# A seventeenth block pair: half of q's projection moved from plain matmuls to seven block products

## The chip, the cores and the metric

The kernel runs on one core of one Trainium2 chip. The metric is the device time of one execution in microseconds (us), as the median of several runs. The profile comes from one further execution, recorded by the hardware profiler.

## What is computed

One layer of a hybrid encoder on 1024 positions of width 1024, in float32. Cut to what matters here:

```python
h = layer_norm(x, emb_ln_g, emb_ln_b)
proj = h @ w_in                       # 1024 x 5120
q, k, v, z_a, u, z_b, g_a, g_b = split(proj)   # q, k, v, z_a, u, z_b: 512 columns each, g_a, g_b: 1024
attn = neighbourhood_attention(q * HEAD_DIM ** -0.5, k, v, rpb)
y_a = attn * silu(z_a)
hh = rg_lru(conv(u), forward) + rg_lru(conv(u), backward)
y_b = hh * silu(z_b)
m = sigmoid(g_a + b_a) * (y_a @ w_ba) + sigmoid(g_b + b_b) * (y_b @ w_bb)
out = layer_norm(ALPHA * h + m @ w_out)
```

The change concerns the projection `h @ w_in`, and of it the 512 columns of q: four column tiles of 128, numbered 0 to 3. The factor 0.125 (HEAD_DIM ** -0.5) is applied when q leaves PSUM.

## The kernel before, in words

**Exact products from two halves.** TensorE works on float32 operands that are rounded to its float32r form. So each operand is split into a high part (a rounding cast) and a low part (the operand less its high part), and a product is the sum of three matmuls: high by high, low by high, high by low (`mm3`, L134). The cast is usually ScalarE's, the subtraction (`lo_of`, L128) VectorE's or GpSimd's.

**Stages.** (1) Eight position tiles of 128 are loaded, normalized, transposed on TensorE and split into the four blocks B11, B12, B21, B22 of the transposed input (the first index is the half of the 1024 input features, the second the half of the 1024 positions). Their block sums T1 to T4 are built from the second half's tiles 4 to 7: `t_full` and `t_last` make them on VectorE (L302 to L310), `t_hi` casts them on ScalarE (L314), `t_lo` makes the low halves on GpSimd (`ht_l<-t,ht_h` in the profile). The block sums lie in a ring of five places of 4 KB per partition (tag `x`) that the loaded tiles used before. (2) In between, V is computed (`v_part`, L328: 24 matmuls for a position tile), stored by `v_hi`, `v_lo`, `v_store`, and q by `q_part(m, n)`: column tile m, position half n, 24 matmuls of 512 columns. `qk_load`, `qk_prep` (`qk_hi` on ScalarE, `qk_lo` on GpSimd) bring the weights of a column tile of q; `q_hi` (ScalarE), `q_lo` (VectorE, L360) and `q_store` bring a finished part away. (3) All other column tiles but V's go through 16 pairs. A pair is two column tiles that are computed together by a Strassen-like scheme: seven block products (`OPS`) of 4 x 3 = 12 matmuls in place of eight. A pair p needs four weight blocks a11, a21, a12, a22 (`s_load`), four sums of them s1 to s4 (`s_sum`, on VectorE, both inputs in SBUF), and high and low parts of seven operands (`s_hi`, `s_lo`). (4) Convolution and gates of the recurrent branch run between the products of the pairs; (5) attention, the two branch products, the output product and the last normalization follow.

**What sets the order.** TensorE, VectorE, ScalarE, GpSimd and SyncE (which issues the DMAs) each execute in the order in which the program issues. In the stage of pairs the order is a table: slot `7 * p + k` holds product k of pair p, with the evacuation of the product before it, the preparation of the next pair and what `todo` holds for that slot (`CONV_AT`, `GATE_AT`, `LATE_AT`, `HEAD_AT` are slot numbers). `evacuate` copies PSUM results to SBUF (u1, u2, u3, on ScalarE) and adds others to them (VectorE); a `take` function per pair says where the four results go: `take_u` for u, `take_zg` for gates, `take_k` for k. A product that accumulates into a PSUM bank waits until the results in it have been read. `U_PAIRS` are the pairs whose last sum goes straight into an SBUF tile, so that they need no fourth bank.

**The boundary.** After V's last part the kernel before computes q(0,1), q(1,1), q(2,0), q(2,1), q(3,0), q(3,1), in this order. Pair 0's loads, sums and splits stand among these six. Then the pools of the first stages are released, VectorE computes a small chain of 128 x 8 operations (a softplus of the recurrence's parameter, L626 to L642, with one ScalarE activation, L629, for which a table is loaded), and pair 0's first product begins. Tile 7's `t_hi` and `t_lo` stand behind q(0,1) and the preparation of q's column tile 2. V's weights lie in the places of the pairs' split operands, so pair 0's high and low parts can't be written before V's last part.

Of the kernel before, what the change touches and what calls it, by code (L numbers as in the profile page):

```python
# [10 lines left out]
F32 = mybir.dt.float32  # L11
F32R = mybir.dt.float32r
AF = mybir.ActivationFunctionType
ALU = mybir.AluOpType

P = 128
# [7 lines left out]
HALF = 512  # L24
# [1 line left out]
EPS = 1e-5  # L26
TWICE = 4.0
C_LRU = 8.0
N_PAIR = 16


WARM = 18, 4, 6
CONV_AT = (7, 24, 45, 66)
GATE_AT = (14, 24, 35, 45, 56, 66, 77, 87)
LATE_AT = (102, 102, 103, 104, 105)
HEAD_AT = 109
LO_POOL = ("a11", "a22")
HI_POOL = ("a12", "s2", "s1", "s3", "s4")
U_PAIRS = (0, 5)
BLOCKS = (1, 0, 6, 2, 3, 4, 5, 7)  # L40
SCORES = (0, 1, 2, 5, 6, 7, 3, 4)
PV_LAG = 3
# [25 lines left out]
def encoder_kernel(ctx, tc, x, gb1, gb, w_qk, w_v, w_s, w_ba, w_bb, w_gate, smalls, bias, w_out, out):  # L68
    nc = tc.nc
    V, A, G, PE, SP = nc.vector, nc.scalar, nc.gpsimd, nc.tensor, nc.sync  # L70
# [10 lines left out]
    wsp = pool("wsp")  # L81
# [15 lines left out]
    q_d = dram.tile([H // 2, P, 2, S], F32, name="q_d")  # L97
    k_d = dram.tile([H // 2, P, 2, S], F32, name="k_d")
    rs_d = dram.tile([H, NT, P], F32, name="rs_d")
    za_d = dram.tile([4, P, S], F32, name="za_d")  # L100
    zb_d = dram.tile([4, P, S], F32, name="zb_d")
# [25 lines left out]
    def lo_of(eng, lo, full, hi):  # L127
        eng.tensor_tensor(lo, full, hi.bitcast(F32), ALU.subtract)  # L128
# [16 lines left out]
    OPS = ("a11", "a12", "s2", "s1", "s3", "s4", "a22")  # L145
    INTO = dict(s2="a11", s3="a11", a22="a11", s4="s1")
    wpl = pool("wpl", "right")
    ln = pool("ln", "right")
# [16 lines left out]
    def qk_load(m):  # L165
        qk_s[m] = wpl.tile([P, NK, P], F32, tag="ws", bufs=1, name=f"wqk{m}_s")
        SP.dma_start(qk_s[m][:], w_qk[m])
# [9 lines left out]
    def qk_prep(m):  # L177
        qk_hi(m)
        qk_lo(m)
# [25 lines left out]
    halves = [slice(c * HALF, (c + 1) * HALF) for c in range(2)]  # L205
# [86 lines left out]
    def t_full(i):  # L292

        tt[i, 3] = wsp.tile([P, 4, P], F32, tag="a22", bufs=2, name=f"t3_{i}")[:]
        t12 = ln.tile([P, 2, 4, P], F32, tag="x", bufs=5, name=f"t12_{i}")
        tt[i, 1], tt[i, 2] = t12[:, 0], t12[:, 1]
        if i in (4, 6):
            tt["last"] = ln.tile([P, 2, 4, P], F32, tag="x", bufs=5, name=f"t4_{i}")
        tt[i, 4] = tt["last"][:, i % 2]
        t1, t2, t3 = (tt[i, c] for c in (1, 2, 3))  # L300
        A.copy(t3, tp4(i, 0))
        V.tensor_tensor(t1, tp4(i, 0), f(B11[0], i), ALU.subtract)  # L302
        V.tensor_tensor(t1, t1, f(B11[1], i), ALU.subtract)
        V.tensor_tensor(t2, tp4(i, 1), t1, ALU.subtract)
        V.tensor_tensor(t3, tp4(i, 1), t3, ALU.subtract)
# [6 lines left out]
    def t_hi(i, *cs):  # L312
        for c in cs:
            A.copy(Ts[c][0][:, :, ti(i)], tt[i, c])  # L314

    def t_lo(i, *cs):
        for c in cs:
            lo_of(G, Ts[c][1][:, :, ti(i)], tt[i, c], Ts[c][0][:, :, ti(i)])
# [3 lines left out]
    def v_part(i, kind, ks):  # L322

        if i not in vos:
            vos[i], vn[i] = bank(f"v{i}"), 0
        for k in ks:
            a = blocks[k // 4][i // 4][kind == "a"][:, k % 4, ti(i)]
            PE.matmul(vos[i][:], a, wv[kind == "w"][k][:], start=vn[i] == 0, stop=vn[i] == 23)  # L328
            vn[i] += 1
# [3 lines left out]
    def v_hi(i):  # L333
        vs = outs["v", i] = ln.tile([P, H, 2, DH], F32R, tag="vs", bufs=2, name=f"vs{i}")
        A.copy(vs[:, :, 0, :], vos[i][:].rearrange("p (h d) -> p h d", d=DH))
# [11 lines left out]
    def q_part(m, n, cols=slice(0, HALF)):  # L347
        if (m, n) not in qos:
            qos[m, n] = bank(f"q{m}_{n}")
        run(mm3(qos[m, n][:, cols], [([t[:, 4 * kk + k, :] for t in qk_w[m]], [t[:, k, cols] for t in blocks[kk][n]])  # L350
                                     for kk in range(2) for k in range(4)]))

    def q_hi(m, n):
        qs = outs["q", m, n] = ln.tile([P, 2, HALF], F32R, tag="vs", bufs=2, name=f"q{m}{n}")
        A.activation(qs[:, 0, :], qos[m, n][:], AF.Copy, scale=0.125)

    def q_lo(m, n):

        qs = outs["q", m, n]
        V.scalar_tensor_tensor(qs[:, 1, :], qos.pop((m, n))[:], 0.125, qs[:, 0, :].bitcast(F32), ALU.mult, ALU.subtract)  # L360

    def q_store(m, n):
        qs = outs.pop(("q", m, n))
        SP.dma_start(q_d[m][:, :, halves[n]], qs[:].bitcast(F32))


    s_a, s_w = {}, {}

    def s_load(p, *names):
        for o in names if p < N_PAIR else ():  # L370
            t = wsp.tile([P, 4, P], F32, tag=o, bufs=2 if o == "a22" else 1, name=f"{o}_{p}f")
            SP.dma_start(t[:], w_s[p, ("a11", "a21", "a12", "a22").index(o)])
            s_a[p, o] = t

    def s_sum(p, *names):
        for o in names if p < N_PAIR else ():
            a, b, op = dict(s1=("a21", "a22", ALU.add), s2=("s1", "a11", ALU.subtract),
                            s3=("a11", "a21", ALU.subtract), s4=("a12", "s2", ALU.subtract))[o]
            t = s_a[p, o] = wsp.tile([P, 4, P], F32, tag=o, name=f"{o}_{p}f")
            V.tensor_tensor(t[:], s_a[p, a][:], s_a[p, b][:], op)  # L380

    def s_hi(p, o):
        if p < N_PAIR:
            s_w[p, o] = pair(wsp, [P, 4, P], f"w{o}_{p}", tag="w" + o)
            (G.tensor_copy if p and o in HI_POOL else A.copy)(s_w[p, o][0][:], s_a[p, o][:])

    def s_lo(p, o):
        if p < N_PAIR:
            hi, lo = s_w[p, o]
            lo_of(G if o in LO_POOL else V, lo[:], s_a[p, o][:], hi[:])  # L390


    K0, K1, KS, BOTH = range(4), range(4, 8), range(8), range(2)
# [136 lines left out]
    v_lo(2)  # L530
    v_store(2)
    keep(5)
    qk_load(2)
    tile_in(4)
    tile_lo(4)
    ln_next(7)
# [41 lines left out]
    t_last(6)  # L578
    t_hi(6, 4)
    t_lo(6, 4)  # L580
    t_full(7)
    for kind in "hwa":
        v_part(6, kind, KS)
# [3 lines left out]
    v_store(6)  # L587
    for kind in "hwa":
        v_part(7, kind, KS)
    v_hi(7)  # L590
    v_lo(7)
    v_store(7)
    s_load(0, "a11")
    for m in range(4):
        for n in BOTH if m > 1 else (1,):
            q_part(m, n)
            if m < 2:
                qk_prep(m + 2)
                if m == 0:
                    qk_load(3)  # L600
                    t_hi(7, 2, 1, 3, 4)
                    t_lo(7, 2, 1, 3, 4)
                    s_load(0, "a21", "a22", "a12")
                else:
                    s_sum(0, "s1", "s2", "s3", "s4")
            q_hi(m, n)
            q_lo(m, n)
            q_store(m, n)
            if m > 1:
                for w in (OPS[:2], OPS[2:4], OPS[4:6], OPS[6:])[2 * (m - 2) + n]:  # L610
                    s_hi(0, w)
                    s_lo(0, w)
    s_load(1, "a11", "a21", "a12", "a22")
    for pl in (ln, wpl, hb12, pst, ps0):
        pl.release()
    psd = tc.alloc_tile_pool(name="psd", bufs=1, space=bass.MemoryType.PSUM, reuse_waits="tile")
# [29 lines left out]
    def take_u(m0):  # L646
        for m in (m0, m0 + 1):
            up = lru.tile([P, S + 3], F32, tag="up", bufs=2, name=f"up{m}")
            V.memset(up[:, 0:2], 0.0)
            V.memset(up[:, S + 2:S + 3], 0.0)  # L650
            ups[m] = up

        def consume(mi, n, add, o):
            dst = gridded(ups[m0 + mi][:, 2:2 + S], n)
            if add is None:
                A.copy(dst, tiled(o[:], 0))
            else:
                V.tensor_tensor(dst, tiled(add[:], 0), tiled(o[:], 0), ALU.add)
            return []
        return consume  # L660

    def take_zg(dst, m0, name, col=None):

        def consume(mi, n, add, o, c=None):
            c = o if c is None else c
            if add is not None:
                V.tensor_tensor(c[:], add[:], o[:], ALU.add)
            z = ev.tile([P, HALF], F32, tag="z", bufs=5, name=f"{name}{m0}{mi}{n}")

            def squash():  # L670
                bias = {} if col is None else dict(bias=smh[:, col + m0 + mi:col + m0 + mi + 1])
                A.activation(z[:], c[:], AF.Tanh, scale=0.5, **bias)

            def store():
                if col is None:
                    V.scalar_tensor_tensor(z[:], z[:], 1.0, c[:], ALU.add, ALU.mult)
                SP.dma_start(dst[m0 + mi][:, n * HALF:(n + 1) * HALF], z[:])
            return [squash, store]
        return consume

    def take_k(m0):
# [216 lines left out]
    def gates_a(j):  # L898
        return lambda: take_zg(ga_d, 2 * j, "ga", SM_BM)

    def gates_b(j):
        return lambda: take_zg(gb_d, 2 * j, "gb", SM_BM + 8)

    takes = [lambda: take_u(0), lambda: take_zg(zb_d, 0, "zb"), lambda: take_zg(za_d, 0, "za"), gates_a(0), gates_a(1),
             lambda: take_u(2), gates_b(0), lambda: take_zg(zb_d, 2, "zb"), gates_a(2), gates_b(1),
             lambda: take_k(0), gates_a(3), lambda: take_k(2), lambda: take_zg(za_d, 2, "za"), gates_b(2), gates_b(3)]
    for t, slot in enumerate(CONV_AT):
# [444 lines left out]
    for i in range(NT):  # L1352
        last = i == NT - 1
        load_z(i + 3)
        z = zs.pop(i)
# [115 lines left out]
```

## Time and profile before

| | us |
|---|---|
| median of 3 runs | 678.17 (678.04 to 678.44) |
| the profiled execution's own time | 678.46 |
| its span, first to last instruction | 676.7 |
| mean granted TensorE clock | 0.997 |

In the profile, PE is TensorE, DVE VectorE, ACT ScalarE, POOL GpSimd, and SPq the queue of SyncE. A row of the timeline has the start in us from the span's beginning, the length in us, engine, line, operation, `out<-in` by the program's names without their numbers, the form, a count, and in brackets the engine's idle time before it with what ended it. Rows of one form that follow each other are merged (x4). A row of waits has the engine and the line that waited, whom it waited for, the total in us, the count and the longest. The chain in order of time lists the work that set the end, piece by piece. A row of the windows has, for a stretch, the busy time of TensorE, its weight loads, VectorE, ScalarE and GpSimd, then the granted clock, the DMA share and GB/s.

### The profile page before, as it was taken

How to read it: one execution, taken by the hardware profiler on the slowest of the kernel's cores; microseconds unless marked ns; L12 is line 12 of the kernel's file. 1: busy time of each engine (PE TensorE's matmuls, PEld its weight loads, DVE VectorE, ACT ScalarE, POOL GpSimd, SP SyncE). 2: the span in 40 equal slices, each digit the busy share in tenths (PEclk: the TensorE clock that was granted, in tenths of full speed). 3: DMA queues.
4: the chain of work that ended last, by engine and by line, in shares of the span. 5: the costliest groups of instructions: out<-in, count | busy, mean ns of one | idle time of the engine just before them, and what ended most of it. 6: DMA issues, size and time to landing. Idle time of an engine off the chain costs nothing.

```text
span 676.7 us, 9344 instructions
## 1 busy us (share of the span) xinstructions
PE 665.2 (98%) x3201; PEld 555.7 (82%) x3201; DVE 492.7 (73%) x821; ACT 364.5 (54%) x612; POOL 355.8 (53%) x258
## 2 busy tenths in 40 slices
PE   8999999999999999999999999999999999999995
PEld 6888888888888887888788888888888878888884
DVE  6978747886998699879967785477787787443434
ACT  6554433256786676669576634477777554210110
POOL 6798632434677576567647444116155456334442
PEclk9999999999999999999999999999999999999998
DMA  8654353233434133431553456998793467412211
GB/s 326 244 179 170 122 206 126 77 110 123 125 128 144 40 103 115 170 126 48 195 178 122 173 191 254 316 366 296 255 323 132 162 220 281 178 62 94 93 63 62
DMA packets 48702, 113.39 MB, mean 168 GB/s; under 512 B 5056, under 2 KB 9744, under 8 KB 47120
## 3 DMA queue, kind: packets, MB, share of 16 engines
q1 hardware_dynamic: 48624, 112.81, 47.2%
q8 instruction: 25, 0.41, 0.3%
q14 instruction: 21, 0.17, 0.1%
q10 hardware_dynamic: 32, 0.01, 0.0%
HBM read 77.11 MB, written 35.68 MB: 167 GB/s over the span
## 4 chain that ended last, share of the span: by engine, by line
PE 89%; DVE 6%; DMA 2%; issue 1%; SPq 1%; ACT 0%; POOL 0%; DVEq 0%; POOLq 0%
PE a L134 30%; PE o L134 13%; PE mb L134 12%; PE s L134 11%; PE q L134 6%; PE v L328 6%; PE acc L1107 3%; PE s L1061 3%; PE pt L1083 3%; PE g L759 2%; DMA wqk_s<-in_w_qk_dram 2%; DVE ws_l L128 1%; PE tp L270 1%; DMA rsb<-rs_d 1%; DVE uc L717 1%
## 5 line engine op out<-in xcount | busy, mean ns | idle before, releaser
L134 PE MATMUL o<-wo_h,ml 128*128 128x512 f32 (+1 forms) x136 | 51.2, 377 | 0.0
L134 PE MATMUL o<-wo_l,mh 128*128 128x512 f32 (+1 forms) x136 | 51.2, 376 | 0.0
L134 PE MATMUL o<-wo_h,mh 128*128 128x512 f32 (+1 forms) x136 | 51.2, 376 | 0.0
L134 PE MATMUL a<-ht_h,ws_h 128*128 128x512 f32 x128 | 50.0, 390 | 0.0
L134 PE MATMUL a<-ht_l,ws_h 128*128 128x512 f32 x128 | 49.8, 389 | 0.0
L134 PE MATMUL a<-ht_h,ws_l 128*128 128x512 f32 x128 | 49.8, 389 | 0.0
L134 PE MATMUL a<-b_h,wa_h 128*128 128x512 f32 x128 | 49.8, 389 | 0.0
L134 PE MATMUL a<-b_h,wa_l 128*128 128x512 f32 x128 | 49.8, 389 | 0.0
L134 PE MATMUL a<-b_l,wa_h 128*128 128x512 f32 x128 | 49.8, 389 | 0.0
L1071 DVE CUSTOM_DVE_ANT_0 sc<-s,bias 128x384 f32<-128x384 f32 (+1 forms) x64 | 33.4, 522 | 21.6 <-PE s L1061 14.2
L1361 DVE SCALAR_TENSOR_TENSOR z<-z,o 128x512 f32<-128x512 f32 (+1 forms) x17 | 11.2, 656 | 51.0 <-PE o L134 51.0
L1091 ACT CAST pt_h<-pt 128x384 fp32r<-128x384 f32 x64 | 29.0, 453 | 25.3 <-PE pt L1083 17.3
L1371 POOL TENSOR_TENSOR z<-z,gb 128x1024 f32<-128x1024 f32 x7 | 16.8, 2400 | 48.5 <-ACT z L1370 48.5
L1076 ACT ACTIVATE p<-sc,summ 128x384 f32<-128x384 f32 (+1 forms) x64 | 37.8, 591 | 5.5 <-DVE summ L1071 5.3
L1340 ACT ACTIVATE sd<-mv,eps_z 128x1 f32<-128x1 f32 x8 | 2.4, 294 | 67.1 <-DVE mv L1366 67.1
L128 DVE TENSOR_TENSOR pt_l<-pt,pt_h 128x384 fp32r<-128x384 f32 x64 | 33.2, 519 | 2.1 <-ACT pt_h L1091 1.6
L328 PE MATMUL v<-wv,b_h 128*128 128x512 f32 x128 | 32.9, 398 | 0.6 <-ACT b_h L279 0.5
L867 POOL CAST wb_h<-wb 128x512 fp32r<-128x512 f32 x9 | 7.0, 779 | 47.4 <-DMA wb<-in_w_bb_dram 47.4
L1061 PE MATMUL s<-ks,qs 128*128 128x384 f32 (+1 forms) x128 | 31.4, 327 | 0.0
L1083 PEld LDWEIGHTS pt<-ident,p 128*128 128x128 f32 x176 | 23.1, 140 | 8.5
L1083 PE MATMUL pt<-ident,p 128*128 128x128 f32 x176 | 29.6, 272 | 0.0
L128 POOL TENSOR_TENSOR wb_l<-wb,wb_h 128x512 fp32r<-128x512 f32 x16 | 22.0, 1375 | 14.3 <-ACT wb_h L865 13.6
(438 smaller groups left out, 2204.2 us busy)
## 6 DMA issues: line engine op xcount, KB each, us to landing
ks<-k_d SPq DMA_DIRECT2D x8, 1024.0 KB, 7.5
h_d<-x SPq DMA_DIRECT2D x8, 512.0 KB, 5.0
v_d<-vs SPq DMA_DIRECT2D x8, 512.0 KB, 3.7
q_d<-q SPq DMA_DIRECT2D x8, 512.0 KB, 3.1
ga_d<-ga SPq DMA_DIRECT2D x16, 256.0 KB, 2.2
gb_d<-gb SPq DMA_DIRECT2D x16, 256.0 KB, 2.6
k_d<-k SPq DMA_DIRECT2D x8, 512.0 KB, 3.4
qs<-q_d SPq DMA_DIRECT2D x8, 512.0 KB, 5.5
```

The source lines that it names most:

```text
L128: eng.tensor_tensor(lo, full, hi.bitcast(F32), ALU.subtract)
L134: PE.matmul(o, a, b, start=first and i == 0, stop=last and i == len(prods) - 1, skip_group_check=not (first and last))
L328: PE.matmul(vos[i][:], a, wv[kind == "w"][k][:], start=vn[i] == 0, stop=vn[i] == 23)
L759: PE.matmul(o[:, n, :], w[:, 2 * d + b, :], us[b][:, n * HALF:(n + 1) * HALF], start=z == 0, stop=z == 1)
L1061: PE.matmul(o[:, :P * len(near(t))], q[:, t * P:(t + 1) * P], k[:, z, keys], start=z == 0, stop=z == 1)
L1071: V.tensor_tensor_reduce(s[:, :w], o[:, :w], heads[h][2][:, b0:b0 + w], -1.0, 3.0e38, ALU.add, ALU.min, accum_out=sums[h][0][:, t:t + 1])
L1076: A.activation(probs[h % 2][t][:], scs.pop((h, t))[:, :w], AF.Exp, bias=sums[h][0][:, t:t + 1], scale=-1.0, accum_out=sums[h][1][:, t:t + 1])
L1083: PE.transpose(tp[:, n * P:(n + 1) * P], probs[h % 2][t][:, z * P:(z + 1) * P], ident[:])
L1091: A.copy(pt[0][:, span(b)], tps[h, b][:, :P * len(near(b))])
L1107: PE.matmul(acc[g][:, d:d + w], vvs[h // 2][:, b, h % 2, :], pt[:, a:a + w], start=b in (1, 6) and z == 0, stop=z == 1 and b == (4, 7)[g])
L1361: V.scalar_tensor_tensor(z[:, cols], z[:, cols], ALPHA * TWICE, o, ALU.mult, ALU.add)
L1371: G.tensor_tensor(z[:], z[:], gb2[:, 0, :], ALU.mult)
```

## The change

q's column tiles 2 and 3 are no longer computed by four `q_part`s of 24 matmuls. They become a pair of their own, with seven products of 12 matmuls, ahead of the sixteen. All slot numbers of the table grow by 7, the pairs' numbers by 1. The new pair 0's weight blocks are loaded earlier, two at a time, into places of the ring `x` (places of dead block sums); the loads of the old pair 0, now pair 1, move up as well. All of the new pair 0's sums, casts and low halves stand within q(0,1) and q(1,1); casts are ScalarE's and low halves VectorE's for this pair. Tile 7's `t_hi` and `t_lo` now stand ahead of `v_hi(7)`. A new `take_q` scales the four results and stores them as `q_store` did.

```diff
-N_PAIR = 16
+N_PAIR = 17
-CONV_AT = (7, 24, 45, 66)
+CONV_AT = (14, 31, 52, 73)
...
-U_PAIRS = (0, 5)
+U_PAIRS = (1, 6)
...
     def s_load(p, *names):
-        for o in names if p < N_PAIR else ():
-            t = wsp.tile([P, 4, P], F32, tag=o, bufs=2 if o == "a22" else 1, name=f"{o}_{p}f")
-            SP.dma_start(t[:], w_s[p, ("a11", "a21", "a12", "a22").index(o)])
+        for z, o in enumerate(names if p < N_PAIR else ()):
+            if p:
+                t = wsp.tile([P, 4, P], F32, tag=o, bufs=2 if o == "a22" else 1, name=f"{o}_{p}f")[:]
+            else:
+                if z == 0:
+                    both = ln.tile([P, 2, 4, P], F32, tag="x", bufs=5, name=f"{o}_{p}f")
+                t = both[:, z]
+            SP.dma_start(t, w_s[p, ("a11", "a21", "a12", "a22").index(o)])
...
-            lo_of(G if o in LO_POOL else V, lo[:], s_a[p, o][:], hi[:])
+            lo_of(G if p and o in LO_POOL else V, lo[:], s_a[p, o], hi[:])
...
     keep(5)
-    qk_load(2)
     tile_in(4)
...
     t_hi(6, 4)
     t_lo(6, 4)
+    s_load(0, "a21", "a22")
+    s_load(0, "a11", "a12")
+    s_load(1, "a21", "a12")
     t_full(7)
...
     for kind in "hwa":
         v_part(7, kind, KS)
+    t_hi(7, 2, 1, 3, 4)
+    t_lo(7, 2, 1, 3, 4)
     v_hi(7)
     v_lo(7)
     v_store(7)
-    s_load(0, "a11")
-    for m in range(4):
-        for n in BOTH if m > 1 else (1,):
-            q_part(m, n)
-            if m < 2:
-                qk_prep(m + 2)
-                if m == 0:
-                    qk_load(3)
-                    t_hi(7, 2, 1, 3, 4)
-                    t_lo(7, 2, 1, 3, 4)
-                    s_load(0, "a21", "a22", "a12")
-                else:
-                    s_sum(0, "s1", "s2", "s3", "s4")
-            q_hi(m, n)
-            q_lo(m, n)
-            q_store(m, n)
-            if m > 1:
-                for w in (OPS[:2], OPS[2:4], OPS[4:6], OPS[6:])[2 * (m - 2) + n]:
-                    s_hi(0, w)
-                    s_lo(0, w)
-    s_load(1, "a11", "a21", "a12", "a22")
+    s_load(1, "a11")
+    s_load(1, "a22")
+    q_part(0, 1)
+    s_sum(0, "s1", "s2", "s3", "s4")
+    for o in OPS[:3]:
+        s_hi(0, o)
+        s_lo(0, o)
+    q_hi(0, 1)
+    q_lo(0, 1)
+    q_store(0, 1)
+    q_part(1, 1)
+    for o in OPS[3:]:
+        s_hi(0, o)
+        s_lo(0, o)
+    q_hi(1, 1)
+    q_lo(1, 1)
+    q_store(1, 1)
...
+    def take_q():
+
+        def consume(mi, n, add, o, c=None):
+            c = o if c is None else c
+            if add is not None:
+                V.tensor_tensor(c[:], add[:], o[:], ALU.add)
+            t = lru.tile([P, 2, HALF], F32R, tag=("us0", "r", "i", "us1")[2 * mi + n], name=f"q2{mi}{n}")
+
+            def high():
+                A.activation(t[:, 0, :], c[:], AF.Copy, scale=0.125)
+
+            def store():
+                V.scalar_tensor_tensor(t[:, 1, :], c[:], 0.125, t[:, 0, :].bitcast(F32), ALU.mult, ALU.subtract)
+                SP.dma_start(q_d[2 + mi][:, :, halves[n]], t[:].bitcast(F32))
+            return [high, store]
+        return consume
...
-    takes = [lambda: take_u(0), lambda: take_zg(zb_d, 0, "zb"), lambda: take_zg(za_d, 0, "za"), gates_a(0), gates_a(1),
+    takes = [take_q, lambda: take_u(0), lambda: take_zg(zb_d, 0, "zb"), lambda: take_zg(za_d, 0, "za"), gates_a(0), gates_a(1),
...
-    heads = [16, 20, 12, 24, 26, 18, 32, 22, 28, 34, 4, 30, 6, 14, 36, 38]
+    heads = [2, 16, 20, 12, 24, 26, 18, 32, 22, 28, 34, 4, 30, 6, 14, 36, 38]
```

More of the change, by code (lines that the diff above doesn't have):

```diff
@@ L28 @@
 C_LRU = 8.0
-N_PAIR = 16
+N_PAIR = 17
 WARM = 18, 4, 6
-CONV_AT = (7, 24, 45, 66)
-GATE_AT = (14, 24, 35, 45, 56, 66, 77, 87)
-LATE_AT = (102, 102, 103, 104, 105)
-HEAD_AT = 109
+CONV_AT = (14, 31, 52, 73)
+GATE_AT = (21, 31, 42, 52, 63, 73, 84, 94)
+LATE_AT = (109, 109, 110, 111, 112)
+HEAD_AT = 116
 LO_POOL = ("a11", "a22")
 HI_POOL = ("a12", "s2", "s1", "s3", "s4")
-U_PAIRS = (0, 5)
+U_PAIRS = (1, 6)
 BLOCKS = (1, 0, 6, 2, 3, 4, 5, 7)
@@ L378, in s_sum @@
                             s3=("a11", "a21", ALU.subtract), s4=("a12", "s2", ALU.subtract))[o]
-            t = s_a[p, o] = wsp.tile([P, 4, P], F32, tag=o, name=f"{o}_{p}f")
-            V.tensor_tensor(t[:], s_a[p, a][:], s_a[p, b][:], op)
+            t = s_a[p, o] = wsp.tile([P, 4, P], F32, tag=o, name=f"{o}_{p}f")[:]
+            V.tensor_tensor(t, s_a[p, a], s_a[p, b], op)
     def s_hi(p, o):
@@ L384, in s_hi @@
             s_w[p, o] = pair(wsp, [P, 4, P], f"w{o}_{p}", tag="w" + o)
-            (G.tensor_copy if p and o in HI_POOL else A.copy)(s_w[p, o][0][:], s_a[p, o][:])
+            (G.tensor_copy if p and o in HI_POOL else A.copy)(s_w[p, o][0][:], s_a[p, o])
     def s_lo(p, o):
```

## The prediction

> **What bounds it now.** I read the page first, then the waits of the TensorE, then the chain that ended last, then the rows around the edit, engine by engine.
>
> ```profile
> span 676.7 us, 9344 instructions
> ...
> PE 665.2 (98%) x3201; PEld 555.7 (82%) x3201; DVE 492.7 (73%) x821; ACT 364.5 (54%) x612; POOL 355.8 (53%) x258
> ...
> PE 89%; DVE 6%; DMA 2%; issue 1%; SPq 1%; ACT 0%; POOL 0%; DVEq 0%; POOLq 0%
> ```
> ```profile
> PE clock L202 <- DVE zero L160: 1.0, 1, 1.0
> ...
> PE a L134 <- DVE w L792: 0.4, 1, 0.4
> ```
> ```profile
> 72.93 32.64 PE q L134 x144
> 105.57 8.16 PE a L134 x36
> ```
> TensorE is the bound: 98% busy, 89% of the chain, and no wait over 1.0 us. The six q parts that the edit touches are one unbroken run, 32.64 / 144 = 0.2267 us per matmul, and pair 0 follows without a gap. So a removed matmul is worth 0.2267 us, and a new TensorE wait costs all of itself. VectorE has 73% on average; what matters is the twenty microseconds before the first product.
>
> **Matmuls.** Out go q(2,0), q(2,1), q(3,0), q(3,1): 4 x 24 = 96. In come 7 x 12 = 84. 12 x 0.2267 = 2.72 us gained. The Trainium skill (TensorE: Matmul & The Clock Gate, "Wait — 56ns, not 53.3ns?") gives 215.7 ns for a warm matmul of 512 columns; by it the gain would be an estimated 2.59 us. The row decides.
>
> **What the removed matmuls covered.** In the kernel before, pair 0's weights were made ready during those 96 matmuls. Now only q(0,1) and q(1,1) lie between the V products and the first product: 48 x 0.2267 = 10.88 us.
>
> ```profile
> 72.77 0.39 PE L134 MATMUL q<-b_h,wqk_h 128*128 128x512 f32 x1
> ...
> 105.41 0.39 PE L134 MATMUL a<-b_h,wa_h 128*128 128x512 f32 x1
> ```
> ```profile
> 100.80 0.69 DVE L360 SCALAR_TENSOR_TENSOR q<-q,q 128x512 fp32r<-128x512 f32 x1 [1.41 <-ACT q L355]
> ```
> By the built program's list of waits the first product waits for VectorE's low half of the q part whose PSUM bank it takes: q(3,0) before, done at 101.49, 3.9 us ahead of 105.41. After, it is q(0,1), and in VectorE's order seven operations of pair 0 (four sums, three low halves) stand in front of it. Without a wait the product would start at 72.77 + 10.88 = 83.65. So the question is when VectorE is through.
>
> ```profile
> 61.08 1.45 DVE L309 TENSOR_TENSOR t<-b_h,t 128x512 f32<-128x512 f32 x1
> 62.56 1.67 DVE L310 TENSOR_TENSOR t<-t,b_l 128x512 f32<-128x512 f32 x1
> ...
> 65.35 0.67 DVE L128 TENSOR_TENSOR vs<-v,vs 128x512 fp32r<-128x512 f32 x1
> ...
> 76.34 0.69 DVE L304 TENSOR_TENSOR t<-tp,t 128x512 f32<-128x512 f32 x1
> ...
> 77.54 0.68 DVE L309 TENSOR_TENSOR t<-b_h,t 128x512 f32<-128x512 f32 x1
> 78.26 0.69 DVE L310 TENSOR_TENSOR t<-t,b_l 128x512 f32<-128x512 f32 x1
> ...
> 89.28 1.85 DVE L380 TENSOR_TENSOR s_0f<-a_0f 128x512 f32<-128x512 f32 x1 [5.33 <-DMA a_0f<-in_w_s_dram]
> ...
> 98.10 1.28 DVE L128 TENSOR_TENSOR ws_l<-s_0f,ws_h 128x512 fp32r<-128x512 f32 x2
> ```
> ```profile
> 60.70 5.94 POOL L128 TENSOR_TENSOR ht_l<-t,ht_h 128x512 fp32r<-128x512 f32 x4 [2.27 <-ACT ht_h L314]
> ...
> 81.91 5.02 POOL L128 TENSOR_TENSOR ht_l<-t,ht_h 128x512 fp32r<-128x512 f32 x4
> ...
> 88.20 2.39 POOL L128 TENSOR_TENSOR wqk_l<-wqk_s,wqk_h 128x1024 fp32r<-128x1024 f32 x1 [1.26 <-ACT wqk_h L171]
> ```
> ```profile
> L128 POOL TENSOR_TENSOR ht_l<-t,ht_h x12: 1277/1295/1747, 60.7 to 85.7; 128x512 fp32r<-128x512 f32 x12
> ```
> The same L309 and L310 take 1.45 and 1.67 us while GpSimd works and 0.68 and 0.69 while it rests. L380 at 89.28 ends at 91.13, 0.54 us after the GpSimd operation that ended at 90.59. So a VectorE operation with both inputs in SBUF waits for the running GpSimd one and ends 0.54 us after it, and GpSimd's next is held (1.75 in place of 1.28). One with a PSUM input (65.35) is not held. Unheld, one follows another after 0.60 us (98.10, two in 1.28), after 0.72 if it needs the result before.
>
> ```profile
> 78.40 1.06 ACT L171 CAST wqk_h<-wqk_s 128x1024 fp32r<-128x1024 f32 x1 [2.57 <-PE q L134]
> 79.37 2.17 ACT L314 CAST ht_h<-t 128x512 fp32r<-128x512 f32 x4
> ...
> 82.63 0.60 ACT L355 ACTIVATE q<-q 128x512 fp32r<-128x512 f32 x1 [1.09 <-DMA v_d<-vs]
> ```
> ```profile
> 79.58 0.36 SPq L342 DMA_DIRECT2D v_d<-vs  x1
> ```
> ```profile
> a_0f<-in_w_s_dram SPq DMA_DIRECT2D x4, 256.0 KB, 5.3
> ```
> **First wait.** An engine starts about 0.04 us after the event it waits for (108.40 to 108.44 in a row below; 0.08 on GpSimd). In the kernel before, tile 7's four casts stand behind qk_prep, at 79.37, and GpSimd's four low halves of them at 81.91. Now nothing stands ahead of the casts but L304, which ends at 77.03: first cast 77.06 to 77.68, first low half ready on GpSimd at 77.76. That is VectorE's busiest stretch.
>
> VectorE's L309 runs 77.54 to 78.22 as now. GpSimd's first low half comes next and ends at 79.40, and L310, ready at 78.26, ends 0.54 later, 79.94 in place of 78.95. The low half of v(6) reads PSUM and ends at 80.54. On ScalarE the fourth cast follows L310 (79.98 to 80.60), and the high half of v(7), which the change moves behind the casts, ends at 81.10; VectorE's low half of it runs 81.14 to 81.82. GpSimd's second low half, held by L310, ends at 81.08, the third at 82.33. Pair 0's first sum s1, ready at 81.74, ends 0.54 after that, 82.87, and holds the fourth to 84.02; s2 needs s1 and ends at 84.56. GpSimd is then done. Six more at 0.60 from 84.48 (s3, s4, the low halves of a11, a12, s2, and q(0,1)'s) end at 88.16, and TensorE starts at 88.20: a wait of 4.55 us, with all of pair 0 queued behind it.
>
> Nothing else is later. Pair 0's four loads go out behind the store at 70.6, take about 5.3 us, and have until 81.7. q(0,1)'s high half needs the store of v(6) landed, which took 3.05 us (79.58 to 82.63): issued at 80.6 it lands at 83.7, while that half's turn on ScalarE comes at 85.1, behind s2's cast. Bounds: with no holding L310 ends at 78.95, v(7)'s low half at 80.82, the eight at 85.75 (0.72 for the one that needs s1), a wait of 2.15; with one more held operation it is 5.6.
>
> ```profile
> 106.73 1.28 ACT L629 ACT_TABLE_LOAD   x1
> 108.44 0.21 ACT L629 ACTIVATE sp<-sp 128x8 f32<-128x8 f32 x1 [0.42 <-DVE sp L628]
> 108.55 0.57 ACT L939 COPY u<-a 128x512 f32<-128x512 f32 x1
> ```
> ```profile
> 108.23 0.17 DVE L628 TENSOR_TENSOR sp<-sm,sp 128x8 f32<-128x8 f32 x1
> 108.68 0.17 DVE L630 TENSOR_SCALAR sp<-sp 128x8 f32<-128x8 f32 x1 [0.27 <-ACT sp L629]
> ...
> 114.09 1.22 DVE L640 SCALAR_TENSOR_TENSOR sp<-sp,sp 128x8 f32<-128x8 f32 x1
> ...
> 115.53 0.69 DVE L380 TENSOR_TENSOR s_1f<-a_1f 128x512 f32<-128x512 f32 x1
> ...
> 116.86 0.68 DVE L658 TENSOR_TENSOR up<-u,a 128x512 f32<-128x512 f32 x1
> ...
> 118.16 1.09 DVE L128 TENSOR_TENSOR wa_l<-a_1f,wa_h 128x512 fp32r<-128x512 f32 x1
> ...
> 120.79 0.68 DVE L658 TENSOR_TENSOR up<-u,a 128x512 f32<-128x512 f32 x1
> ```
> **Second and third wait.** VectorE still owes four low halves and q(1,1)'s (five at 0.60 from 88.08, to 91.16), and only then the softplus chain, which in the kernel before began at the boundary. Its third operation ends 0.4 later, 91.56. In the built program the activation table load now stands behind that one, where before it was free (106.73): load to 92.88, activation to 93.08, copy u1 to 93.6. The third product, due at 88.20 + 24 x 0.2267 = 93.64, just misses a wait.
>
> From L630 (now 93.12) to the next pair's first sum it is 6.85 us, 108.68 to 115.53, of which L640, held behind GpSimd, took 1.05 too many: 5.8 without. With the same holding, since GpSimd's work for the next pair comes in the same place, the sums begin at 99.97. The pair's first add ended 2.01 after that (116.86 + 0.68 - 115.53): 101.98. ScalarE's new scaled copy of q waits for this add, 0.60 long, and behind it in the queue stands copy u3, which ends at 103.1. The sixth product needs u3 and is due at 88.20 + 60 x 0.2267 = 101.80: a wait of 1.35. The second add ended 5.94 after the sums began; with the new low half of q ahead of it, 6.54: 106.51. The seventh product needs it and is due 2.72 after the sixth began, 105.87: a wait of 0.7. Together 2.05. If VectorE is not held here (1.05 less in the chain, 0.8 in two operations like that at 118.16), u3 ends at 102.05, the add at 104.66, and 0.25 is left of both.
>
> **Hidden.** The same megabyte is loaded (four of 256 KB for two of 512). On SyncE's queue six loads now pass ahead of the stores of v(6) and v(7); begun at 71 and issued within 3 us, they are out before v(6)'s half is made. Pair 1's other two follow v(7)'s store at 82, where before they went at 108. qk_prep(2) and (3) leave ScalarE and GpSimd, which only helps. The loads of pair 2 go out about 5 us later against the pair, behind the store of q, and VectorE waits for them inside pair 1, where sixteen operations (10 to 17 us) have 19 us until pair 1's seventh product; if that cover failed the wait would be 1 or 2 us. Pairs 1 to 16 keep the old slots, so the 0.4 us wait stays.
>
> **Sum.** -2.72 + 4.55 + 1.35 + 0.70 = +3.9 us. The profiled execution took 678.46 (span 676.7) and would take 682.4; the median of the runs is 0.29 lower, so 682.1.
>
> **Rivals.** Half clock:
>
> ```profile
> 668.00:671.00 3.00, 0.72 (x7) 0.52 (x5) 2.14 (x8) 0.29 (x1) 0.00 (x0) 1.00 0.35 139
> ...
> 672.00:673.00 1.00, 0.00 (x0) 0.00 (x0) 1.00 (x4) 0.00 (x0) 0.00 (x0) 0.76 0.00 0
> ```
> After the last matmul (668.72) the granted clock falls to half at 672.52 (0.76 in that microsecond), after 3.8 us idle. A wait of 4.55 may be enough. A half-clock stretch of 3.8 us would lose 1.9, inside the 2.05 that VectorE sets anyway: nothing. One twice as long loses 3.8, of which 1.75 show: 683.8; 0.12. The Trainium skill (same page, "Part 1: The HAM clock gate") says that an idle window of about 3.4 us on a free-running raster halves the clock; the row agrees, and by its raster a 4.55 us gap would hold a whole window about one time in three.
>
> VectorE absorbs the later waits: 4.55 + 0.25 - 2.72 = +2.1, 680.3. For it: only three held operations make them; against it: GpSimd meets VectorE there in the rows too. 0.15.
>
> Not slower: VectorE and GpSimd do not hold each other, so a first wait of 2.15 and no others: -0.57, 677.6. It decides from the point where q(0,1)'s low half is done by 83.65 + 2.72 = 86.37, 1.8 us ahead of my sum, and needs L310, s1 and s2 at 0.7 us each; against it stands every row above in which the two engines meet. 0.05. That the boundary has no wait at all, 675.5, needs VectorE through by 83.65, 2.1 us earlier than even its unheld queue allows: 0.03.
>
> **Chances.** The forecast 0.65, the rivals 0.12, 0.15, 0.05, 0.03. Changes under 0.2% (1.36 us) can't be told from none here. Slower: 0.92; same: 0.05; faster: 0.03. Range 680.0 to 683.8: the two rivals that are slower, the lower one less 0.3 for what my start times may be off.
>
> **What would show it.** In the profile after: an idle TensorE of 4 to 5 us ahead of the first "a" product, released by VectorE's L360; L310 of tile 7 at about 1.7 us; two shorter waits some 14 to 18 us later, on ScalarE's u copy and VectorE's add; 12 matmuls fewer. It is wrong if TensorE runs through the boundary, if GpSimd's low halves of tile 7 still start after 80, or if the first wait ends on a DMA.

## The result: 4.05 us slower, by one wait and a stretch of half clock

The changed kernel took 682.33 us (median of 6 runs, 682.11 to 682.85), the kernel before 678.28 (6 runs): a ratio of 1.0061, with a 95% interval of 1.0049 to 1.0073. 682.1 was forecast, so the sum came out right. One of the three waits behind it did as told; the other two did not appear, and something else of the same size stood in their place.

First the top of the page of the changed kernel, and the first and the fifth line of its TensorE waits.

```profile
span 680.4 us, 9354 instructions
...
PE 664.8 (98%) x3189; PEld 555.4 (82%) x3189; DVE 501.8 (74%) x835; ACT 365.1 (54%) x615; POOL 354.3 (52%) x261
```
```profile
PE a L134 <- DVE q L360: 4.5, 1, 4.5
...
PE a L134 <- DVE w L814: 0.3, 1, 0.3
```
The 12 matmuls are gone (3189 for 3201), and TensorE has a wait of 4.5 us that the kernel before did not have, released by VectorE's low half of q, L360. It is the only new wait in the list. VectorE's rows up to it, and GpSimd's beside them:

```profile
77.45 0.68 DVE L309 TENSOR_TENSOR t<-b_h,t 128x512 f32<-128x512 f32 x1
78.17 1.67 DVE L310 TENSOR_TENSOR t<-t,b_l 128x512 f32<-128x512 f32 x1
...
81.61 1.17 DVE L385 TENSOR_TENSOR s_0f<-a_0f 128x512 f32<-128x512 f32 x1
82.82 1.66 DVE L385 TENSOR_TENSOR s_0f<-s_0f,a_0f 128x512 f32<-128x512 f32 x1
...
87.41 0.68 DVE L360 SCALAR_TENSOR_TENSOR q<-q,q 128x512 fp32r<-128x512 f32 x1
```
```profile
77.67 6.26 POOL L128 TENSOR_TENSOR ht_l<-t,ht_h 128x512 fp32r<-128x512 f32 x4 [2.09 <-ACT ht_h L314]
```
L310, s1 and s2 are each as long as the running GpSimd low half makes them (1.67, 1.17, 1.66 where 0.69 is free), and L360 ends at 88.09. The chain of the changed kernel goes on from there:

```profile
87.49 0.61 DVE q L360
88.10 0.04 issue
88.14 10.64 PE a L134 x36
98.78 2.72 PE s L134 x12
101.50 2.72 PE a L134 x12
104.22 2.72 PE s L134 x12
106.94 10.88 PE a L134 x48
```
The first 36 matmuls of pair 0 take 10.64 us, where 36 x 0.2267 is 8.16; after them pair 0 runs without a gap. By the starts of the matmuls 2.32 us are lost, 2.28 of them in the first product alone (88.14 to 93.14 where 2.72 is due), and none at the sixth or seventh, where the forecast had its second and third wait. The cause stands in a view of four stretches of 3.41 us, cut so that the changes of the clock fall on their edges (length, TensorE's busy time and matmuls, granted clock, DMA share, GB/s):

```profile
82.55:85.96 3.41, 1.07 (x5) 1.00 1.03 330
85.96:89.37 3.41, 1.23 (x3) 0.50 0.07 25
89.37:92.79 3.42, 3.42 (x9) 0.50 0.54 201
92.79:96.20 3.41, 3.41 (x16) 1.00 0.29 107
```
The clock was granted at half from 85.96 to 92.79. Nine matmuls fit where sixteen do behind it. From pair 0's start at 88.14 to 92.79 are 4.65 us, half of which, 2.3, is lost.

### The profile page after: what moved, and what is told of

Same layout as the page of the kernel before. It is cut to its first block, busy times and chain, and to the rows that moved or that the text cites. A ratio compares the mean times of both kernels' runs of the same rounds, so it can differ in the third digit from the quotient of the medians.

```text
span 680.4 us, 9354 instructions
## 1 busy us (share of the span) xinstructions
PE 664.8 (98%) x3189; PEld 555.4 (82%) x3189; DVE 501.8 (74%) x835; ACT 365.1 (54%) x615; POOL 354.3 (52%) x261
## 4 chain that ended last, share of the span: by engine, by line
PE 81%; DVE 9%; POOL 3%; DMA 2%; issue 2%; ACT 1%; SPq 1%; DVEq 0%; POOLq 0%
PE a L134 32%; PE o L134 13%; PE mb L134 13%; PE s L134 12%; PE acc L1129 4%; PE s L1083 3%; PE pt L1105 3%; DMA wqk_s<-in_w_qk_dram 2%; POOL x L259 2%; PE g L781 2%; DVE ws_l L128 1%; DVE wa_l L128 1%; DVE b_l L128 1%; POOL ht_l L128 1%; DVE uc L739 1%
## 5 line engine op out<-in xcount | busy, mean ns | idle before, releaser
L134 PE MATMUL a<-b_h,wa_h 128*128 128x512 f32 x136 | 54.1, 398 | 4.5 <-DVE q L360 4.5
L134 PE MATMUL a<-b_h,wa_l 128*128 128x512 f32 x136 | 53.8, 396 | 0.0
L134 PE MATMUL a<-b_l,wa_h 128*128 128x512 f32 x136 | 53.6, 394 | 0.0
L134 PE MATMUL a<-ht_h,ws_h 128*128 128x512 f32 x136 | 53.1, 390 | 0.0
L134 PE MATMUL a<-ht_h,ws_l 128*128 128x512 f32 x136 | 53.0, 390 | 0.0
L134 PE MATMUL a<-ht_l,ws_h 128*128 128x512 f32 x136 | 52.9, 389 | 0.0
L134 PEld LDWEIGHTS a<-b_h,wa_h 128*128 128x128 f32 x136 | 26.1, 192 | 10.4 <-DVE q L360 4.9
L134 PEld LDWEIGHTS a<-b_l,wa_h 128*128 128x128 f32 x136 | 26.1, 192 | 5.6
L134 PEld LDWEIGHTS a<-b_h,wa_l 128*128 128x128 f32 x136 | 26.1, 192 | 5.5
```

The costliest lines, as they stand in the source:

```text
L134: PE.matmul(o, a, b, start=first and i == 0, stop=last and i == len(prods) - 1, skip_group_check=not (first and last))
```

## The experiments

Each was run beside the kernel before on the same chip (the last on another chip than the rest). The times of the kernel before scattered more there (677.4 to 679.9 over 42 runs) than in the runs above; stage 1 alone reached q(0,1) anywhere from 72.6 to 73.5 us. So ratios are given with intervals, and in the traces two stretches are compared that stage 1 does not touch: from the first matmul of q(0,1) to pair 0's first, less the 48 x 0.2267 = 10.88 us of q(0,1) and q(1,1) (the first wait), and from pair 0's first matmul to pair 1's, less the 84 x 0.2267 = 19.04 us of its own matmuls (lost inside pair 0). These two come from one profiled execution of each kernel.

| kernel | first wait | lost inside pair 0 | ratio, 95% interval |
|---|---|---|---|
| changed | 4.68 | 2.32 | 1.0061 (1.0049 to 1.0073) |
| twenty spare matmuls | filled | 2.16 | 1.0074 (1.0060 to 1.0088) |
| softplus moved | 4.59 | 1.73 | 1.0058 (1.0042 to 1.0074) |
| both | filled | 0.13 | 1.0033 (1.0021 to 1.0044) |
| no GpSimd low halves of tile 7 | 2.17 | 2.22 | 1.0027 (1.0017 to 1.0036) |
| early loads, q first, softplus moved | 0 | 0.62 | 0.9975 (0.9965 to 0.9984) |
| the same, softplus ahead of pair 0 | 0 | 6.69 | 1.0055 (1.0042 to 1.0067) |
| order alone, softplus moved | 0 | 0.69 | 0.9975 (0.9966 to 0.9984) |
| early loads, sums together | 0 | 0.00 | 0.9958 (0.9944 to 0.9971) |

**Twenty spare matmuls in the wait.** Is the half clock a cost, or does it lie inside what VectorE sets anyway?

```
     q_part(1, 1)
+    spare = pst.tile([P, HALF], F32, tag="bank", name="spare")
+    for _ in range(20):
+        PE.matmul(spare[:], B11[0][:, 0, :P], B11[0][:, 0, :], start=True, stop=True)
```


> Twenty matmuls of 512 columns into a spare PSUM bank, whose result nobody reads, stand between q(1,1) and pair 0: 20 x 0.2267 = 4.53 us, so they fill the first wait and little more. The first product should still start at about 88.1, released by VectorE's low half of q(0,1), but the clock should stay whole. Theory A (VectorE's queue sets the end of pair 0, and the half clock lies inside it): the sixth product is then due at 88.14 + 13.60 = 101.74, but ScalarE's copy u3 ended at 103.22, a wait of 1.5; the seventh is due 2.72 later, 105.98, and the second add ended at 106.15, a wait of 0.2. Together 1.7 in place of the 2.4 that the half clock took: 681.6, 0.7 less than the changed kernel. Theory B (the half clock is a cost of its own): 2.4 less, 679.9, with no wait at the sixth product. Theory C (the clock does not hang on the idle time): as the changed kernel, 682.3.

The clock stayed whole, and nothing was gained. Its two new TensorE waits, the matmuls that end them, and ScalarE's copy u3:

```profile
PE s L134 <- ACT u L970: 1.1, 1, 1.1
...
PE a L134 <- DVE c L694: 0.3, 1, 0.3
```
```profile
103.17 0.58 ACT L970 COPY u<-s 128x512 f32<-128x512 f32 x1
```
```profile
103.80 0.50 PE L134 MATMUL s<-b_h,ws_h 128*128 128x512 f32 x1 [1.07 <-ACT u L970]
...
107.16 0.50 PE L134 MATMUL a<-ht_h,wa_h 128*128 128x512 f32 x1 [0.33 <-DVE c L694]
```
Pair 0 began at 88.83 (q(0,1) had begun 0.68 later than in the changed kernel's trace). Its sixth product was due 60 x 0.2267 = 13.60 later, at 102.43, and began at 103.80, 1.37 late, when u3 was there. The seventh was due at 106.52 and began at 107.16, 0.64 late, when VectorE's second add was. The prediction had 1.35 and 0.70 for these two. Theory B, 679.9, is out: its time would be 2.4 below the changed kernel, and this one was not below it at all. So is theory C, as the clock did stay whole. Theory A named the right two waits, but its time, 681.6 (a ratio of 1.0049), lies below the interval. In the traces 0.16 less is lost inside pair 0 than in the changed kernel, where it expected 0.7 less; the ratio reads 0.9 us above the changed kernel's, which the two intervals allow.

**Softplus moved**, in six pieces into pairs 1 and 2, `smh` alone left in its place:

```
-    V.tensor_scalar(t0[:], lam, -1.0, None, ALU.mult)
...
-    V.tensor_scalar(nsp[:], t0[:], -C_LRU, None, ALU.mult)
...
+    for c in range(6):
+        at(9 + c, 1, lambda c=c: softplus(c))
```


> The softplus chain (27 small VectorE operations, the activation and its table load) is moved from ahead of pair 0 into pairs 1 and 2, in six pieces. Pair 1's sums and pair 0's adds then start some 8 us earlier on VectorE. Theory A: the first wait of 4.5 stays and the half clock with it; what VectorE frees is not on the path while TensorE runs at half clock, so 682.3, as the changed kernel (within 0.3). Theory D (the softplus chain ahead of the adds sets the end of pair 0 in the changed kernel): 2.0 less, 680.3.

The first wait and the half clock stayed, and 1.73 us were lost inside pair 0: in this execution one stretch of half clock, with TensorE busy all through it, 3.41 / 2 = 1.71.

```profile
82.78:86.20 3.42, 1.77 (x8) 1.00 1.02 313
86.20:89.61 3.41, 0.63 (x3) 1.00 0.24 90
89.61:93.02 3.41, 3.41 (x10) 0.50 0.41 154
```
The ratio is the changed kernel's. Theory D, which wanted 680.3 (680.3 / 678.28 = 1.003), is out.

**Both edits.**

> Both edits at once: the twenty matmuls that keep TensorE busy through the first wait, and the softplus chain in pairs 1 and 2. Theory A: neither the half clock nor VectorE's later adds hold pair 0, so only the first wait is left: 4.5 - 2.72 = +1.8 on the kernel before, 680.0, 2.3 less than the changed kernel and less than the two single gains together. Theory B: the same as with the twenty matmuls alone, 679.9. Theory D: the same as with the softplus chain moved alone, 680.3, or 2.4 below that, 677.9, if the half clock adds to it.

The chain has no step but TensorE's:

```profile
83.98 4.53 PE spare L615 x20
88.52 8.30 PE a L134 x36
96.82 2.72 PE s L134 x12
99.54 2.72 PE a L134 x12
102.26 2.72 PE s L134 x12
104.98 10.88 PE a L134 x48
```
Only 0.13 us are left inside pair 0 (its first matmul is followed by the second 0.33 later instead of 0.23). Neither edit alone gained anything that could be told from nothing; the two together gain what theory A said: it had 680.0, a ratio of 1.0025, inside the interval. The time of this run alone would fit theories B and D too (679.9 and 680.3); it is the two single runs that rule them out. Half clock and VectorE's queue each set pair 0's end at nearly the same time, and taking away one uncovers the other.

**GpSimd's low halves of tile 7 left out.**

```
     tile_lo(5)
+    for c in Ts:
+        G.memset(Ts[c][1][:, :, ti(7)].bitcast(F32), 0.0)
...
     t_hi(7, 2, 1, 3, 4)
-    t_lo(7, 2, 1, 3, 4)
```


> GpSimd's four low halves of tile 7 are left out (those quarter tiles are zeros, written some 20 us before), so GpSimd has nothing to do from 75.6 until pair 1's weights; VectorE's queue is the same. Theory A (GpSimd's work holds VectorE): L310 takes 0.69 in place of 1.66, s1 and s2 0.69 each, VectorE ends the low half of q(0,1) at about 85.6 and the first wait is 2.1 us. That is too short for the half clock; VectorE's softplus chain and adds move up with the start, so the two later waits of together 1.7 to 2.05 come in its place: -2.72 + 2.1 + 1.9 = +1.3 on the kernel before, 679.6. Theory E (VectorE's queue is as long without GpSimd): the first wait stays 4.5 and the time 682.3. If the later waits do not come, 677.7.

TensorE's wait and VectorE's rows ahead of it:

```profile
PE a L134 <- DVE q L360: 2.0, 1, 2.0
```
```profile
78.74 0.69 DVE L310 TENSOR_TENSOR t<-t,b_l 128x512 f32<-128x512 f32 x1
...
81.21 0.68 DVE L385 TENSOR_TENSOR s_0f<-a_0f 128x512 f32<-128x512 f32 x1
81.93 0.69 DVE L385 TENSOR_TENSOR s_0f<-s_0f,a_0f 128x512 f32<-128x512 f32 x1
...
85.55 0.68 DVE L360 SCALAR_TENSOR_TENSOR q<-q,q 128x512 fp32r<-128x512 f32 x1
```
With the same queue, the three held operations take 0.68 to 0.69, and the first wait is 2.17 in place of 4.68. So half of it is GpSimd's holding, the other half the length of the queue; theory E is out. The Trainium skill (SBUF — State Buffer, "SBUF: two separate sides") has this as a lock on a shared port pair: of VectorE, with two inputs in SBUF, and GpSimd, the one that starts first has it for its whole instruction. These rows agree (0.69 without GpSimd's work, 1.67 beside it). One part of the expectation missed: a wait of 2.0 us was held too short for the half clock, and it was not.

```profile
84.17:87.58 3.41, 1.40 (x7) 1.00 0.50 177
87.58:91.00 3.42, 3.42 (x10) 0.50 0.53 201
```
Of the 2.22 lost inside pair 0 it took 1.71; the seventh product then still began 0.24 late, when the second add was through (104.59).

**Early loads, q(0,1) first, softplus moved.** The core of the edit; q(0,1)'s halves take one of the five places of `x` in place of one that waits for the store of v(6):

```
     t_full(6)
+    s_load(0, "a21", "a22")
+    s_load(0, "a11", "a12")
...
     t_last(6)
+    for o in OPS[:2]:
+        s_hi(0, o)
+        s_lo(0, o)
...
-    t_hi(7, 2, 1, 3, 4)
+    q_part(0, 1)
+    t_hi(7, 2, 1, 3)
+    q_hi(0, 1, "x", 5)
+    q_lo(0, 1)
+    q_store(0, 1)
+    t_hi(7, 4)
     t_lo(7, 2, 1, 3, 4)
     v_hi(7)
     v_lo(7)
```


> All the causes named so far are taken out of the changed kernel. Pair 0's four loads go out 4.5 us earlier, behind the store of v(4); the casts and low halves of a11 and a12 stand ahead of tile 7's blocks (VectorE rested from 73.55 to 74.80 there); q(0,1)'s halves stand ahead of v(7)'s, in a place of their own that needs no earlier store; and the softplus chain lies in pairs 1 and 2. Theory A: VectorE is through with the low half of q(0,1) at about 81, ahead of 83.6, so TensorE runs through the boundary, the clock stays whole, and pair 0 has no wait inside: only the 12 matmuls are left, -2.72, a ratio of 0.996 to the kernel before. Rival F (the seventeenth pair has a price that no queue explains, such as its loads or its stores): the ratio stays at 1.000 or above though the first wait is gone.

The boundary ran through and the clock stayed whole: faster than the kernel before, at 0.9975, but not the 0.996 that was expected. Rival F is out. Of the missing part, about 1 us, 0.62 lies inside pair 0, where the third product waited for ScalarE's u1 (0.3 in the list of waits, due 89.8, u1 done at 90.2):

```profile
89.13 0.59 ACT L355 ACTIVATE q<-q 128x512 fp32r<-128x512 f32 x1
89.62 0.58 ACT L975 COPY u<-a 128x512 f32<-128x512 f32 x1
```
**The same with the softplus chain ahead of pair 0.**

> As the run before, but with the softplus chain back ahead of pair 0. Theory A: no first wait, TensorE starts pair 0 at about 83.6; but VectorE ends pair 0's low halves at about 88.6, the activation's table load ends at 90.3, so ScalarE's copy u1 ends at about 91 and the third product (due 89.1) waits 2; pair 1's sums begin at about 97, the first add ends at 99, u3 at 100.1, the sixth product (due 97.25) starts there at the earliest and the seventh waits for the add at 103.4. All waits inside pair 0 together 3.4: as much as is saved, +0.7 on the kernel before, 1.001. Rival B (the first wait and its half clock are the whole loss): 0.996, as the run before.

Theory A had the direction and the place, but only half the size: 6.69 us lost inside pair 0, not 3.4.

```profile
PE a L134 <- ACT u L966: 3.7, 1, 3.7
```
```profile
90.96 1.28 ACT L639 ACT_TABLE_LOAD   x1 [1.79 <-DVE sp L638]
92.25 0.21 ACT L639 ACTIVATE sp<-sp 128x8 f32<-128x8 f32 x1
92.37 0.57 ACT L966 COPY u<-a 128x512 f32<-128x512 f32 x1
```
```profile
88.54:91.95 3.41, 0.74 (x4) 1.00 0.07 25
91.95:95.36 3.41, 2.37 (x6) 0.50 0.37 134
95.36:98.78 3.42, 3.42 (x10) 0.50 0.01 2
98.78:102.19 3.41, 3.41 (x17) 1.00 0.00 0
```
VectorE reached the chain 2 us later than worked out, so the table load ended at 92.24 and not 90.3, and the third product began at 92.99, 3.87 behind its due time of 89.12. That wait brought two stretches of half clock, 98.78 - 92.99 = 5.79 us with work, 2.90 lost. 3.87 + 2.90 is 6.77, the loss within 0.1. With the first wait gone this is as slow as the changed kernel: the chain ahead of pair 0 is a cause by itself. Here it acts by the activation and its table load, which stand ahead of ScalarE's u1 and wait for the chain's third operation; no run moves these two without the rest of the chain. Rival B is out.

**Order alone, softplus moved:** the same order of q(0,1), a11 and a12, but pair 0's loads where the changed kernel has them.

> Only orders are changed: pair 0's loads stay where the changed kernel has them; the two halves of q(0,1), in a place of their own, and the casts and low halves of a11 and a12 stand ahead of v(7)'s halves and of pair 0's four sums; the softplus chain lies in pairs 1 and 2. Theory A: L310 is still held (79.8), then v(6)'s low half, q(0,1)'s at 81.0, a11's and a12's, each held by one of GpSimd's low halves, at 81.6 and 82.8: done ahead of 83.6, no wait at the boundary, 0.996. Rival G (without earlier loads something else is late: the loads, or tile 7's casts): a wait of 1 to 2 us at the boundary, 0.998 to 0.999.

No wait at the boundary, and the same ratio as with early loads, 0.9975: nothing here waited for the loads. Rival G is out. The 0.996 was missed again, because 0.69 is lost at the third product, which waited for ScalarE's u1 (0.4 in the list of waits). VectorE's low half of q(0,1), and the two of a11 and a12:

```profile
81.15 0.67 DVE L360 SCALAR_TENSOR_TENSOR q<-q,q 128x512 fp32r<-128x512 f32 x1
81.75 2.37 DVE L128 TENSOR_TENSOR wa_l<-a_0f,wa_h 128x512 fp32r<-128x512 f32 x2
```
The two took 2.37 where 1.28 is free, so they were held, and the second ended at 84.12, later than the 82.8 of the expectation. 0.85 of that is stage 1's (q(0,1) began at 73.43, not 72.58); pair 0 began at 84.31 and does not need the second one for another 2.72 us.

**Early loads, sums together.** The edit is against the run with early loads:

```
-    s_sum(0, "s1", "s2")
-    for o in OPS[2:3]:
-        s_hi(0, o)
-        s_lo(0, o)
-    s_sum(0, "s3", "s4")
+    s_sum(0, "s1", "s2", "s3", "s4")
```


> The run with the earlier loads, with one more change of order: pair 0's four sums stand together, ahead of the low half of s2, which kept VectorE idle for 0.7 us while it waited for ScalarE's cast. Then s4 ends at about 86.9 in place of 88.05, ScalarE's last casts and q(1,1)'s high half end 1.1 us earlier, and its copy u1 ends at about 89.1 in place of 90.2, ahead of the third product (due 0.2267 x 24 = 5.44 after pair 0's start, 89.8). Theory A: the third product's wait goes, and pair 0 takes the 19.04 us from its first product to pair 1's that the pairs behind it take, 0.6 less: a ratio of 0.9966 to the kernel before, and all of the 2.72 us in the trace between the first q matmul at 73 and pair 1. Rival H (the sixth or seventh product then waits instead, for the copy u3 or the second add): no gain, 0.9975.

```profile
73.68 10.88 PE q L134 x48
84.56 8.16 PE a L134 x36
92.72 2.72 PE s L134 x12
95.44 2.72 PE a L134 x12
98.16 2.72 PE s L134 x12
100.88 10.88 PE a L134 x48
```
q(0,1), q(1,1) and pair 0 now run as one, each matmul at 0.2267 us. The time is 676.00 us against 678.95 for the kernel before on the same chip. The ratio of 0.9958 (0.9944 to 0.9971) is 2.85 us, with an interval of 2.0 to 3.8, which holds the 2.72 of the twelve matmuls. This version beats both kernels. That it beats the two runs at 0.9975 only the traces show (0.00 lost for 0.62 and 0.69), since the intervals overlap. It takes both edits. The run of order alone has its sums together as well; it differs from this one only in pair 0's loads and in the place of the splits of a11 and a12. With early loads these splits stand ahead of tile 7's blocks, and not in VectorE's queue at the boundary, where the two low halves took 2.37.

## Why the prediction was right

**Twelve matmuls, -2.72: right.** The last run, in which nothing else is left, shows it in full.

**First wait, 4.55: right, and for the reason given.** The wait was 4.5 in the list, 88.14 - 83.46 = 4.68 by the stretch. The prediction's times were L310's end 79.94, v(7)'s low half 81.82, s1 82.87, s2 84.56, L360 88.16; the trace has 79.83, 81.70, 82.79, 84.48, 88.09. The start without a wait was put at 83.65; TensorE was 0.19 earlier there. That GpSimd's holding is half of it (2.15 without, by the lower bound) was shown by leaving its low halves out: 2.17.

**Second and third wait, 1.35 and 0.70: the mechanism and the sizes were right, but the clock stood in their place.** They appeared, at 1.37 and 0.64, as soon as TensorE was kept busy through the first wait. In the changed kernel the half clock delayed the second and all later products by 2.3. The sixth began at 104.06 and the seventh at 106.78; u3 was done at 103.21 and the second add at 106.16, before either. That they are one cause, the softplus chain ahead of the adds, is shown by the pair of runs that moves it: alone no gain, with the spare matmuls 2.0.

**The half clock came, and its chance was too low.** The prediction had one stretch of 3.8 us as costing nothing, inside the 2.05, and one twice as long as a rival at 0.12 with 683.8. What came lies between the two: 6.83 us at half clock, of which 4.65 had work in them. That it does not add to the later waits but covers them was right: 2.32 was lost against 2.05 expected, 0.3 more. The step that failed is the one that read the end of the kernel before, 3.8 us idle ahead of the drop, as the idle time that is needed, and with the Trainium skill (TensorE: Matmul & The Clock Gate, "Part 1: The HAM clock gate") took a whole idle window of 3.4 us to be the condition, so one time in three. The trace disagrees with that rule: each drop inside the work came at the end of a stretch of 3.41 us in which TensorE had still been busy for 1.07, 0.63, 1.40 or 0.74 us. So part of the number is luck. Its last 2.05 stood for two waits that did not happen, and the half clock cost about as much. Less of it would have let those waits show, 2.16 by the run with spare matmuls; two stretches full of work would have cost 3.4.

**What it sums to.** Up to pair 1's first matmul the forecast had +3.9: -2.72 + 4.55 + 1.35 + 0.70. The traces have -2.72 + 4.68 + 2.32 = 4.28, less the 0.19 by which the execution reached q(0,1) earlier. The last matmul is 3.50 later (672.22 for 668.72). Up to 540 us, past the pairs, the lag grows to 4.4; then 0.9 is given back in one place, where the kernel before waits for VectorE's `ya_l` (541 to 542 us, 0.3 in its list of waits) and the changed kernel does not. Why it does not was not looked into.

**Hidden work: right.** No wait of the changed kernel at the boundary ended on pair 0's loads or on a store. VectorE waited 4.6 us for pair 2's loads inside pair 1, as told, and TensorE ran on. The early loads gained only at the end, where their 0.69 came from making room in VectorE's queue and not from a wait for them.

## What to carry to other kernels

When a step is taken out, ask what the engines behind it did in its time: here the 96 matmuls of q that went (21.8 us) had covered VectorE's preparation of pair 0. Under the 10.9 us that were left 4.7 stuck out, and the order of that preparation, not its amount, was the loss. Before ranking two causes of a loss, take them away one at a time and then together; each alone gained nothing here, because either one set the same end. A change that reads slower may be a gain held back by order alone: with q's halves first, the first weights loaded and split earlier, the sums together and a chain of small operations out of the way it became 0.9958.

## What the runs showed of the hardware that was not expected

A short wait is enough to halve TensorE's clock, and what counts is how busy a fixed stretch of 3.41 us was. Stretches with 0.63, 0.74, 1.07 and 1.40 us of work (18 to 41% of 3.41) were followed by one at half clock; one with 1.77 us (52%) was not, nor any fuller one at full clock in these four traces. The stretches are fixed in time. From the drops at 85.96 (changed), 89.61 (softplus moved), 87.58 (no low halves) and 91.95 (softplus ahead of pair 0), 171 to 173 steps of 3.4133 us lead to 676.46, 676.70, 674.67 and 675.62. After the last matmul the clock dropped again at 676.47, 676.70, 674.68 and 675.63, worked out from the mean clock of half a microsecond. So a wait of 2.0 us cost 1.7 us more, while part of a wait of 4.4 lay in a stretch that counted as busy. To come back took a stretch with work throughout: one with 2.37 us (69%) at half clock was followed by another at half. Where the stretches begin differed between executions, so the same wait can cost one of them or two.
